# Attention's block mask: written into PSUM by VectorE, in place of a product of mask tiles on TensorE

## The chip, the cores and the metric

The kernel runs on one core of one Trainium2 chip. A core has TensorE (matrix products, PE in the profile; PEld is its weight loads), VectorE (DVE), ScalarE (ACT), GpSimd (POOL) and SyncE (SP), which issues most of the loads. TensorE writes into PSUM, which VectorE and ScalarE read and write; the other operands lie in SBUF. The metric is device time in microseconds (us) from start to end of one execution; less is better.

## The reference

Two layers of a streaming encoder on x of shape (1, 1024, 1024). The first mixes by a gated short convolution, the second by latent attention with 8 heads; each is followed by a squared-ReLU MLP of 4096. What matters here is the attention with its mask. Queries come in blocks of 128 rows and see keys in chunks of 64: a row of chunk c sees chunks 0 to c.

```python
for i in range(S // Q_BLOCK):
    q0, k_end = i * Q_BLOCK, (i + 1) * Q_BLOCK
    ...
    q_chunk = np.arange(q0, k_end) // CHUNK
    k_chunk = np.arange(k_end) // CHUNK
    mask = k_chunk[None, :] <= q_chunk[:, None]
    s = jnp.where(mask[None, None], s, jnp.finfo(jnp.float32).min)
    p = jax.nn.softmax(s, axis=-1).astype(v.dtype)
    outs.append(jnp.einsum("bhqk,bkhd->bqhd", p, v[:, :k_end]))
```

With Q_BLOCK 128 and CHUNK 64, keys beyond the block are never computed, and of the keys of a block's own 128 columns only one square is masked: the first 64 rows of the block do not see its last 64 columns.

## The kernel before

All large products are split into a high and a low part, and three products of such parts stand for one (`mm`, line 173). The program's stages follow each other: convolution layer, its MLP, the shared keys and values, attention, output projection, second MLP. Attention runs from about 1145 to 1431 us of the profile.

Attention loops over the heads h = 0 to 7, and in each over blocks i = 7 down to 0 of 128 queries. `scores(i, ...)` computes one block for one head into `sp`, a PSUM tile of up to 1024 columns (two banks, named big in the profile, of which there are two). For each bank of 512 columns there are five products (line 1433): rotary and plain parts, high and low. Then one more product is added onto the last 64 columns (line 1434). Its operands are two constant tiles: `mask_l`, 128 x 128, of which row 0 is 1 in columns 0 to 63, and `mask_r`, 128 x 64, of which row 0 is -2^127. It adds -2^127 to the first 64 rows of the last 64 columns and 0 to the others. VectorE takes the negated row maximum (line 1436), ScalarE the exponential with its row sum (line 1439), and `end()`, called later, the reciprocal of the sum and the scaling of the row (lines 1443 and 1444). The scaled rows p are turned by TensorE (`turn`, transposes on line 1459), evicted in a high part by ScalarE (1462) and a low part by VectorE (1463), and multiplied with the values.

Between the blocks stand the keys, queries, rotary parts and values of the next head, and the modulation sums of the second layer (`ada_acc`, line 198 on VectorE, which add up rows of a weight as they are loaded).

The source sets the order of the calls. In stretches marked `pinned` it is kept on the engines; elsewhere, in attention too, a planner orders each engine's instructions by what is ready in its own reckoning, with the source's order as priority.

`mask_l` and `mask_r` are filled once, by two casts (lines 1103 and 1104) from `cs`, a tile of constants loaded at the start (line 136), which also holds the identity for the transposes. The host writes the constants (`_consts`): identity, the two mask pieces, then the tables of cosines and sines.

Of the kernel before, what the change touches and what calls it, by code (L numbers as in the profile page):

```python
# [9 lines left out]
F32R = mybir.dt.float32r  # L10
# [7 lines left out]
P = 128  # L18
# [4 lines left out]
HALF = 512  # L23
CHUNK = 64
# [9 lines left out]
MASKED = -(2.0 ** 127)  # L34
# [19 lines left out]

VEC_ROWS = 109
BIAS_ROWS = 112
C_ID, C_ML, C_MR, C_T = 0, 128, 256, 320
C_COLS = 2368


@with_exitstack
def trunk_kernel(ctx: ExitStack, tc: tile.TileContext, x, c, ada_w, ada_b, norm_g, conv_in_w, conv_w,
                 conv_b, conv_out_w, kv_ada_w, kv_ada_b, kv_norm_g, kv_a_w, kv_a_norm_g, kv_b_w,
                 q_a_w, q_a_norm_g, q_b_w, attn_o_w, mlp_up_w, mlp_down_w, consts, out):
    nc = tc.nc
    uid = [0]

    def nm(s):
        uid[0] += 1
        return f"{s}_{uid[0]}"  # L70

    def pool(name, side="left", **kw):
        return tc.alloc_tile_pool(name=name, bufs=1, side=side, reuse_waits="tile", **kw)

    cp = pool("cp")
# [24 lines left out]
    def big_ps():  # L100
        return wide[0].tile([P, 2 * HALF], F32, tag="big", name=nm("big"))
# [4 lines left out]
    def small(w=1):  # L106
        return cp.tile([P, 8], F32, tag="small", name=nm("small"), bufs=16)[:, :w]
# [22 lines left out]
    cs = cp.tile([P, C_T], F32, name="cs")  # L130
# [33 lines left out]
        return vecs[:, (l * 4 + v) * 8:(l * 4 + v) * 8 + 8]  # L164

    V_CW, V_CB, V_KV, V_QA, V_KA = 64, 88, 96, 104, 107

    mask_l = cp.tile([P, P], F32R, name="mask_l")
    mask_r = cp.tile([P, CHUNK], F32R, name="mask_r")

    def mm(out_, lhs, rhs, first, last, more=False):
        for i, (a, b) in enumerate(((1, 0), (0, 1), (0, 0))):
# [740 lines left out]
    def conv_phase():  # L913
# [77 lines left out]
        def weights(k, m):  # L991

            raw = ad.tile([P, D], F32, tag=("acc", "gmb")[k % 2], name=nm("w"), bufs=1)[:, :3 * P]
            ld(raw.rearrange("p (g m) -> p g m", g=3),
               conv_in_w[0][k * P:(k + 1) * P, :].rearrange("p (g c) -> p g c", g=3)[:, :, m * P:(m + 1) * P])
            w = [wr.tile([P, 3 * P], F32R, tag="w" + part_, name=nm("w"), bufs=6) for part_ in "hl"]
            split_w(w[0], w[1], raw)
            return w
# [56 lines left out]
        with pinned([mybir.EngineType.PE, mybir.EngineType.SP]):  # L1055
            load_x(0)
            aw = [ada(0)]
            w = [weights(0, 0)]
# [27 lines left out]
            w = w[KD]  # L1086
# [7 lines left out]
            for k in range(KD):  # L1094
                w, w_ = weights(k + 1, 1) if k < KD - 1 else None, w
# [4 lines left out]
            evict(1, acc)  # L1100
        wr.release()
        up = pool("up", "right")
        nc.vector.tensor_copy(mask_l, cs[:, C_ML:C_ML + P])
        nc.vector.tensor_copy(mask_r, cs[:, C_MR:C_MR + CHUNK])

        def triple(j):
            keep = {}
# [44 lines left out]
    bg += ada_fm(ad, "s0f", w0, 4 * D, 32, gain(0, 2))  # L1152
    bg += ada_fm(ad, "h0f", w0, 3 * D, 24)
    conv_phase()

    def down_phase(slots, sizes, wd, src_fn, g, xsrc, xdst, next_w, key, ys=None, pairs=True):
# [262 lines left out]
    def scores(i, K, Q, r_):  # L1419

        n = (i + 1) * P
        qs = slice((i % 4) * P, (i % 4 + 1) * P)
        q = Q[i // 4]
        r_ = r_[i // 4]
        sp = big_ps()
        for b in range((n + HALF - 1) // HALF):
            w = min(HALF, n - b * HALF)
            o_ = sp[:, b * HALF:b * HALF + w]
            kp = [t_[:, b * HALF:b * HALF + w] for t_ in kk]
            ops = [(r_[:, qs], kp[1]), (q[1][:, qs], K[b][0][:, :w]), (r_[:, qs], kp[0]), (q[0][:, qs], K[b][1][:, :w]),  # L1430
                   (q[0][:, qs], K[b][0][:, :w])]
            for j, (a, m_) in enumerate(ops):
                nc.tensor.matmul(o_, a, m_, start=j == 0, stop=j == 4 and b * HALF + w < n)  # L1433
        nc.tensor.matmul(sp[:, n - CHUNK:n], mask_l, mask_r, start=False, stop=True)
        mx = small()
        nc.vector.tensor_reduce(mx, sp[:, :n], AX.X, ALU.max, negate=True)
        pt = at.tile([P, n], F32, tag=f"p{i}", name=nm("p"), bufs=1)
        l_ = small()
        nc.scalar.activation(pt, sp[:, :n], AF.Exp, bias=mx, accum_out=l_)

        def end():
            rl = small()
            nc.vector.reciprocal(rl, l_)
            nc.vector.tensor_scalar(pt, pt, rl, None, op0=ALU.mult)

        return pt, end
# [56 lines left out]
    for h in range(H):  # L1503
# [5 lines left out]
        run_bg(5)  # L1509
        pts = {}  # L1510
        pts[7], end = scores(7, K, Q, r_)
        if before:
            before.turn(2)
        else:
            values(V, kw0, 0)
            values(V, kw0, 1)
        end()
        pts[6], end = scores(6, K, Q, r_)
        if before:
            before.turn()  # L1520
            before.mul(3)
        else:
            values(V, kw0, 2)
            values(V, kw0, 3)
        end()
        pts[5], end = scores(5, K, Q, r_)
        if more:
            qw_ = q_weights(raw_q, h + 1)
# [77 lines left out]
def _consts():  # L1606
    import numpy as np
    k = np.zeros((P, C_COLS), np.float32)
    k[:, C_ID:C_ID + P] = np.eye(P)
    inv = (np.float32(1.0) / np.power(np.float32(10000.0), np.arange(0, ROPE, 2, dtype=np.float32) / np.float32(ROPE)))  # L1610
    ang = np.arange(S, dtype=np.float32)[None, :] * inv.astype(np.float32)[:, None]
    cos, sin = np.cos(ang).astype(np.float32), np.sin(ang).astype(np.float32)
    k[:, C_T:C_T + S] = np.concatenate([cos] * 4)
    k[:, C_T + S:] = np.concatenate([-sin, sin] * 2)
    k[0, C_ML:C_ML + CHUNK] = 1.0
    k[0, C_MR:C_MR + CHUNK] = MASKED
    return k


# [20 lines left out]
```

## Time and profile before

| what | value |
|---|---|
| three runs | median 2179.61 us, 2178.7 to 2180.36 |
| the profiled execution | 2180.9 us |
| its span, first to last instruction | 2179.1 us |
| mean granted TensorE clock | 0.993 |

The page gives busy time by engine, the span in slices, the DMA queues, the chain of work that ended last, and the costliest groups of instructions. In a row such as "L1436 DVE TENSOR_REDUCE small<-big" stand the source line, the engine, the operation, and the tiles written and read. "x64 | 42.8, 686 | 7.8 <-ACT pt L1462 7.6" are the number of instructions, their busy time in us, the mean length of one in ns, and the idle time of the engine just before them with what ended most of it. A row of the timeline has start, length, engine, line, operation; a row of the chain has start, length on the chain, engine and line. "ACT p L1439 <- DVE small L1436" is a row of the waits: who waited for whom, us in total, times, longest.

### The profile page before, as it was taken

The page shows a single profiled execution, that of the slowest core. Times are in us where ns is not written, and L with a number is a line of the kernel's source. Part 1 is how long each engine was busy: PE and PEld are TensorE (multiplying, and loading weights), DVE is VectorE, ACT ScalarE, POOL GpSimd, SP SyncE. Part 2 cuts the span into 40 slices and gives each one's busy share as a digit, 9 for nine tenths or more (in the row PEclk, how much of TensorE's full clock was granted, in tenths as well). Part 3 has the DMA queues.
Part 4 walks back from the last instruction along what each step waited for, and adds up shares of the span by engine and source line. Part 5 has one row for each costly group of instructions (what it writes and reads, how often), then busy time and mean ns, then how long its engine had stood idle before and what let it go on. Part 6 is the DMA issues. An engine that isn't in the chain of part 4 may idle for free.

```text
span 2179.1 us, 25354 instructions
## 1 busy us (share of the span) xinstructions
PE 2098.4 (96%) x9702; PEld 1726.9 (79%) x9702; DVE 1512.0 (69%) x2001; ACT 1062.7 (49%) x1512; POOL 4.0 (0%) x8
## 2 busy tenths in 40 slices
PE   6999999989999999999899999999989999999998
PEld 5888878768888778888777888877768887788887
DVE  5877776967665578956788776665966665458556
ACT  4533354735454434344665555564735444444342
POOL 0000000000000000000000000000000000000000
PEclk9999999999999999999999999999999999999999
DMA  8344463346543977444224131053345553853243
GB/s 243 101 147 134 145 212 127 101 146 203 184 160 120 330 262 254 167 147 170 78 69 122 66 113 44 25 164 122 98 149 174 183 188 119 312 196 126 97 145 135
DMA packets 242335, 330.95 MB, mean 152 GB/s; under 512 B 18629, under 2 KB 143906, under 8 KB 242214
## 3 DMA queue, kind: packets, MB, share of 16 engines
q1 hardware_dynamic: 204328, 248.57, 35.8%
q10 hardware_dynamic: 37886, 80.77, 9.8%
q8 instruction: 76, 1.25, 0.2%
q14 instruction: 45, 0.37, 0.1%
HBM read 248.55 MB, written 80.74 MB: 151 GB/s over the span
## 4 chain that ended last, share of the span: by engine, by line
PE 69%; DVE 14%; ACT 8%; DMA 6%; issue 2%; SPq 0%; ACTq 0%; DVEq 0%
PE one L173 34%; PE mm L173 18%; PE tp L173 7%; PE big L173 4%; DMA raw<-in_ada_w_dram 3%; ACT junk L258 2%; PE big L1433 2%; DVE y L318 1%; DVE raw L319 1%; DVE acc L198 1%; PE tp L1459 1%; DVE uplo L177 1%; DMA raw<-ha 1%; DVE y L312 1%; ACT small L260 1%
## 5 line engine op out<-in xcount | busy, mean ns | idle before, releaser
L173 PE MATMUL one<-slot,uphi 128*128 128x512 f32 x1240 | 383.9, 391 | 0.0
L173 PEld LDWEIGHTS one<-slot,uphi 128*128 128x128 f32 x1240 | 233.8, 189 | 48.6 <-issue 0.5
L173 PE MATMUL big<-slot 128*128 128x512 f32 x1152 | 266.5, 391 | 1.0 <-ACT y L884 0.6
L173 PE MATMUL one<-slot,uplo 128*128 128x512 f32 x620 | 244.1, 394 | 14.6 <-DVE y L580 12.6
L173 PEld LDWEIGHTS big<-slot 128*128 128x128 f32 x1152 | 215.9, 188 | 46.7 <-ACT y L884 1.4
L173 PE MATMUL one<-ring,ring 128*128 128x512 f32 x1008 | 232.3, 391 | 6.5 <-DVE ring L177 6.5
L177 DVE TENSOR_TENSOR uplo<-raw,uphi 128x1024 fp32r<-128x1024 f32 x121 | 145.8, 1221 | 130.5 <-ACT uphi L176 130.5
L176 ACT ACTIVATE ring<-w 128x1024 fp32r<-128x1024 f32 x98 | 103.7, 1058 | 261.7 <-PE tp L173 132.1
L173 PEld LDWEIGHTS one<-ring,ring 128*128 128x128 f32 x1008 | 188.2, 188 | 49.5 <-ACT ring L176 5.8
L176 ACT ACTIVATE uphi<-raw 128x1024 fp32r<-128x1024 f32 x121 | 128.2, 1060 | 143.8 <-PE one L173 91.6
L177 DVE TENSOR_TENSOR ring<-w,ring 128x1024 fp32r<-128x1024 f32 x98 | 119.8, 1222 | 109.7 <-ACT ring L176 109.6
L173 PE MATMUL mm<-ring,ring 128*128 128x512 f32 x672 | 162.4, 390 | 0.0
L173 PE MATMUL tp<-ring,ring 128*128 128x512 f32 x672 | 161.7, 389 | 0.0
L173 PE MATMUL mm<-slot,uphi 128*128 128x512 f32 x504 | 158.5, 395 | 0.0
L173 PEld LDWEIGHTS one<-slot,uplo 128*128 128x128 f32 x620 | 116.8, 188 | 43.6 <-DVE y L580 15.1
L173 PEld LDWEIGHTS mm<-ring,ring 128*128 128x128 f32 x672 | 125.7, 188 | 27.1 <-DVE ring L177 0.6
L173 PEld LDWEIGHTS tp<-ring,ring 128*128 128x128 f32 x672 | 126.2, 188 | 26.2
L198 DVE SCALAR_TENSOR_TENSOR acc<-raw,csil,acc 128x1024 f32<-128x1024 f32 x88 | 112.8, 1282 | 45.7 <-DMA raw<-in_ada_w_dram 42.2
L177 DVE TENSOR_TENSOR ring<-raw,ring 128x1024 fp32r<-128x1024 f32 x98 | 119.4, 1219 | 18.3 <-ACT ring L176 18.3
L173 PE MATMUL one<-slot,s 128*128 128x512 f32 x468 | 115.1, 395 | 3.7 <-DVE s L177 3.7
L578 ACT ACTIVATE y<-one 128x512 f32<-128x512 f32 x62 | 36.7, 592 | 159.3 <-PE one L173 104.7
L173 PEld LDWEIGHTS mm<-slot,uphi 128*128 128x128 f32 x504 | 95.3, 190 | 20.3 <-issue 1.4
(278 smaller groups left out, 3498.4 us busy)
## 6 DMA issues: line engine op xcount, KB each, us to landing
ha<-y ACTq DMA_DIRECT2D x196, 256.0 KB, 3.6
raw<-ha SPq DMA_DIRECT2D x98, 512.0 KB, 4.2
raw<-in_ada_w_dram SPq DMA_DIRECT2D x80, 512.0 KB, 4.5
raw<-in_mlp_up_w_dram SPq DMA_DIRECT2D x70, 512.0 KB, 4.2
w<-in_mlp_down_w_dram SPq DMA_DIRECT2D x56, 512.0 KB, 4.9
raw<-hd SPq DMA_DIRECT2D x24, 512.0 KB, 5.3
xs<-raw ACTq DMA_DIRECT2D x24, 512.0 KB, 2.9
raw<-xs SPq DMA_DIRECT2D x24, 512.0 KB, 3.2
```

The source lines that it names most:

```text
L173: nc.tensor.matmul(out_, lhs[a], rhs[b], start=first and i == 0, stop=last and i == 2, skip_group_check=more)
L176: nc.scalar.activation(hi, src, AF.Copy)
L177: nc.vector.tensor_tensor(lo, src, hi.bitcast(F32), op=ALU.subtract)
L198: nc.vector.scalar_tensor_tensor(acc, raw, s, acc, op0=ALU.mult, op1=ALU.add)
L258: nc.scalar.activation(junk, src, AF.Square, accum_out=ss)
L260: nc.scalar.activation(rt, ss, AF.Sqrt, bias=eps_d)
L312: nc.vector.tensor_tensor(y, y, p_, op=ALU.add)
L318: nc.vector.scalar_tensor_tensor(y, y, rroot(ss), self.gmb, op0=ALU.mult, op1=ALU.mult)
L319: nc.vector.tensor_tensor(xr, xr, y, op=ALU.add)
L578: nc.scalar.activation(dst, x_, AF.Copy)
L1433: nc.tensor.matmul(o_, a, m_, start=j == 0, stop=j == 4 and b * HALF + w < n)
L1459: nc.tensor.transpose(p_[:, c:c + P], pts[4 * hf + i][:, j * P:(j + 1) * P], ident)
```

## The change

The product on line 1434 goes. In its place VectorE writes -2^127 into the masked square (64 rows, the last 64 columns) of the scores in PSUM, after the products and ahead of the row maximum. The two mask tiles, their casts and their place in the constants go too, so that `cs` has 128 columns instead of 320. Which of the five products carries the stop mark changes with it.

```diff
-C_ID, C_ML, C_MR, C_T = 0, 128, 256, 320
-C_COLS = 2368
+C_ID, C_T = 0, 128
+C_COLS = 2176
...
-    mask_l = cp.tile([P, P], F32R, name="mask_l")
-    mask_r = cp.tile([P, CHUNK], F32R, name="mask_r")
...
-        nc.vector.tensor_copy(mask_l, cs[:, C_ML:C_ML + P])
-        nc.vector.tensor_copy(mask_r, cs[:, C_MR:C_MR + CHUNK])
...
             for j, (a, m_) in enumerate(ops):
-                nc.tensor.matmul(o_, a, m_, start=j == 0, stop=j == 4 and b * HALF + w < n)
-        nc.tensor.matmul(sp[:, n - CHUNK:n], mask_l, mask_r, start=False, stop=True)
+                nc.tensor.matmul(o_, a, m_, start=j == 0, stop=j == 4)
+        nc.vector.memset(sp[:CHUNK, n - CHUNK:n], MASKED)
         mx = small()
         nc.vector.tensor_reduce(mx, sp[:, :n], AX.X, ALU.max, negate=True)
...
-    k[0, C_ML:C_ML + CHUNK] = 1.0
-    k[0, C_MR:C_MR + CHUNK] = MASKED
```

## The prediction

> **What bounds the kernel now.** I read the head of the page and its chain, then the busy time by stage, then the lines of the mask, then single instructions around them.
>
> ```profile
> span 2179.1 us, 25354 instructions
> PE 2098.4 (96%) x9702; PEld 1726.9 (79%) x9702; DVE 1512.0 (69%) x2001; ACT 1062.7 (49%) x1512; POOL 4.0 (0%) x8
> PE 69%; DVE 14%; ACT 8%; DMA 6%; issue 2%; SPq 0%; ACTq 0%; DVEq 0%
> ```
>
> The kernel is bound by TensorE: 96% busy, 69% of the chain that ended last. The change touches one stage, attention, and a few instructions in the first microseconds. The busy time by stretch (us busy, instructions in brackets; PE, PEld, DVE, ACT, POOL) shows attention whole, its first head, and an inner head:
>
> ```profile
> 1145.00:1431.00 286.00, 274.27 (x1579) 232.63 (x1578) 215.00 (x385) 157.34 (x315) 0.00 (x0) 1.00 0.22 71
> 1145.00:1170.00 25.00, 20.72 (x121) 17.57 (x119) 24.81 (x36) 14.73 (x25) 0.00 (x0) 1.00 0.47 136
> 1232.00:1263.00 31.00, 30.76 (x182) 26.69 (x181) 22.48 (x44) 16.74 (x34) 0.00 (x0) 1.00 0.10 32
> ```
>
> Attention lasts 286 us. The inner head is TensorE's (30.76 of 31). The first head is VectorE's (24.81 of 25). So the change, which takes work from TensorE and gives work to VectorE, gains in some places and loses in others, and the sum has to be made place by place on the chain.
>
> **What is removed on TensorE.** The answer for the line of the mask product:
>
> ```profile
> L1434 PE MATMUL big<-mask_r,mask_l x64: 191/193/246, 1152.0 to 1430.5; 128*128 128x64 f32 x64
> ```
>
> There are 64 products, eight in each of eight heads. Their 193 ns is a latency. What they cost a stream is seen from one start to the next. TensorE alone, narrow stretches of the timeline (start us, length us):
>
> ```profile
> 1238.59 0.19 PE L1434 MATMUL big<-mask_r,mask_l 128*128 128x64 f32 x1
> 1238.62 0.47 PE L173 MATMUL mm<-ckT,kw 128*128 128x512 f32 x1
> 1238.93 0.39 PE L173 MATMUL mm<-ckT,kw 128*128 128x512 f32 x1
> 1239.16 0.40 PE L173 MATMUL mm<-ckT,kw 128*128 128x512 f32 x1
> ...
> 1245.12 0.19 PE L1434 MATMUL big<-mask_r,mask_l 128*128 128x64 f32 x1
> 1245.15 0.30 PE L1459 MATMUL tp<-cs,p 128*128 128x128 f32 x1
> 1245.29 0.38 PE L1459 MATMUL tp<-cs,p 128*128 128x128 f32 x2
> 1247.75 0.60 PE L1459 MATMUL tp<-cs,p 128*128 128x128 f32 x4
> ```
>
> The product behind the mask starts 0.03 us after it, but the one after that only 0.31 later, where the ordinary step of these 512-column products is 0.23 (1238.93 to 1239.16). So a mask costs 0.03 + 0.31 - 0.23 = 0.11 us: a 64-column product is too short to hide the next weight load. Ahead of a transpose it costs 0.03 + 0.14 - 0.11 = 0.06 us, the ordinary step of transposes being (0.60 - 0.38) / 2 = 0.11, from the rows of four and of two.
>
> The Trainium skill, TensorE: Matmul & The Clock Gate, section Part 2 (step 1, and the table under Back-to-back issue gap), has the next weights load while the present product runs, and a product of up to 64 columns at about 60 cycles with a floor near 25 ns. The trace agrees for the start of the next product and not for the one after it. An estimate by that page is 34 x 25 ns = 0.9 us where the rows below give 3.1.
>
> The chain inside attention passes through the mask product 34 times; first and last:
>
> ```profile
> 1172.20 0.03 PE big L1434
> ...
> 1425.52 0.03 PE big L1434
> ```
>
> Of these, 20 stand ahead of a wide product and 14 ahead of a transpose (counted in the timeline): 20 x 0.11 + 14 x 0.06 = 3.0 us gained. The other 30 lie where TensorE waits for something else soon after, or is behind another engine, and I take them at nothing. If all 54 whose next product starts within 0.1 us counted (34 wide, 20 transposes), the gain would be 34 x 0.11 + 20 x 0.06 = 4.9 us; that is the upper end.
>
> **What is added on VectorE.** Sixty-four memsets of 64 x 64 into PSUM, each right ahead of a row maximum. The trace has no memset into PSUM. The nearest rows are the memsets into SBUF, and the row maximum itself, which touches PSUM:
>
> ```profile
> L154 DVE MEMSET ones<- x1: 165/165/165, 0.8 to 0.8; 128x128 f32 x1
> L156 DVE MEMSET eps_d<- x1: 59/59/59, 0.9 to 0.9; 128x1 f32 x1
> ...
> L1436 DVE TENSOR_REDUCE small<-big 128x1 f32<-128x256 f32 x8 | 3.3, 409 | 0.0
> L1436 DVE TENSOR_REDUCE small<-big 128x1 f32<-128x128 f32 x8 | 2.3, 282 | 0.0
> ```
>
> Between the memset rows, 64 columns take 59 + 63 x 106 / 127 = 112 ns; that is the value I take, being the same operation. Above, the maximum shrunk to 64 columns takes 282 - 127 / 2 = 219 ns. Below, 59 ns. The maximum reads what the memset writes, so it waits for it. What such a pair and a free pair cost:
>
> ```profile
> 1237.08 0.16 DVE L1443 RECIPROCAL small<-small 128x1 f32<-128x1 f32 x1 [0.17 <-ACT p L1439]
> 1237.28 0.69 DVE L1444 TENSOR_SCALAR p<-p,small 128x896 f32<-128x896 f32 x1
> ...
> 1241.58 0.68 DVE L1387 TENSOR_TENSOR k<-mm,k 128x512 fp32r<-128x512 f32 x1
> 1242.18 0.81 DVE L1436 TENSOR_REDUCE small<-big 128x1 f32<-128x640 f32 x1
> ```
>
> A dependent instruction starts 0.04 us after the end of the one before (1237.24 to 1237.28), an independent one 0.08 before it (1242.26 to 1242.18). The memset takes the maximum's old place behind the earlier work, so it puts the maximum back by 0.11 + 0.04 = 0.15 us; at the upper bound 0.26; at the lower end, 59 ns overlapped by 0.08, nothing. The chain passes through the maximum 21 times, and that is where it counts; the first, and groups in which it stands between a reciprocal and its scaling, the first and last of seven (the last is the last maximum too):
>
> ```profile
> 1154.81 0.98 DVE small L1436
> ...
> 1159.47 0.07 DVE small L1443
> 1159.54 0.99 DVE small L1436
> 1160.53 0.66 DVE p L1444
> ...
> 1422.05 0.16 DVE small L1443
> 1422.21 0.59 DVE small L1436
> 1422.80 0.47 DVE p L1444
> ```
>
> So 21 x 0.15 = 3.2 us lost; bounds 0 and 21 x 0.26 = 5.5 us. At the other 43 the cover is VectorE's idle time in the stage, 286 - 215 = 71 us; without that cover all 64 would cost 9.6 us. Behind the waiting memset stand the maximum, the reciprocal and scaling of the tile before, and the splits of the turned tiles; ScalarE's exponential waits for the maximum, and TensorE's transposes for the scaling.
>
> The Trainium skill, VectorE: DVE Perf Modes, section The TRN2 errata, gives an operation from PSUM 120 cycles plus one per element at 0.96 GHz, which would be 192 ns here if writing to PSUM costs the same. An estimate by that page is 21 x (0.19 + 0.04) = 4.8 us in place of 3.2. No row of this trace shows the operation.
>
> **What moves at the start.** Two casts go, and the first load carries 128 columns instead of 320.
>
> ```profile
> L1103 DVE CAST mask_l<-cs x1: 227/227/227, 3.2 to 3.2; 128x128 fp32r<-128x128 f32 x1
> L1104 DVE CAST mask_r<-cs x1: 186/186/186, 3.4 to 3.4; 128x64 fp32r<-128x64 f32 x1
> ...
> 7.42 0.17 DVE L180 TENSOR_SCALAR csil<-csil 128x8 f32<-128x8 f32 x1 [3.86 <-ACT csil L151]
> 8.38 0.41 PE L936 MATMUL tp<-cs,raw 109*128 109x109 f32 x1 [8.38 <-DMA raw<-in_kv_a_norm_g_dram]
> ```
>
> VectorE idles 3.86 us behind the casts, and TensorE's first product waits for another load until 8.38. Nothing is gained; without that cover it would be the 0.4 us of the two casts. The tiles behind move by 1.5 KB in each partition, which I put at nothing, as the size of no tile that is worked on changes.
>
> **Sum.** -3.0 + 3.2 = +0.2 us, which is no change. The profiled execution took 2180.9 us, 1.8 outside its span, and lies 1.3 above the median of the runs shown, 2179.61. On the profiled execution the sum is 2181.1, on the median 2179.8. With both bounds the case reaches from -4.9 to -3.0 + 5.5 = +2.5: 2174.7 to 2182.1.
>
> **The rivals.** The casts stand at 3.2 us although their line comes after the convolution: the order on an engine is set by a planner that works with its own times, not by the source. That is where the other cases come from.
>
> Slower, by one mechanism: something is put between the memset and its maximum. The planner does so with the reciprocal and its scaling whenever other work is ready (seven of the 21 places above). The piece it would find most often is a split of a turned tile:
>
> ```profile
> L1463 DVE TENSOR_TENSOR pt<-tp,pt 128x512 fp32r<-128x512 f32 x64 | 42.8, 686 | 7.8 <-ACT pt L1462 7.6
> ...
> ACT p L1439 <- DVE small L1436: 43.2, 39, 2.1
> DVE acc L198 <- DMA raw<-in_ada_w_dram: 8.0, 6, 3.1
> ```
>
> Each such place puts the exponential back by 0.69 us, and ScalarE already waits 43.2 us for the maxima, 39 times. At seven places on the chain that is 4.8 us, with the sum above +5.0: 2184.6; at ten, +7.1: 2186.7. It decides from seven places (4.4 us is 0.2%). Against it: where the chain is pure VectorE work, the order inside it costs nothing.
>
> Faster: the memsets fall into the pauses that dependent pairs leave, and cost nothing on the chain, and the shifted order spares the modulation sums one of their waits for a load (last row: 8.0 us in six waits, longest 3.1). Then -3.0 - 3.1 = -6.1: 2173.5. For it: in the group at 1159.47 a memset could stand in the reciprocal's shadow. Against it: these waits hang on buffers that VectorE itself frees, and later work frees them later.
>
> The mask was cheap: the weight load behind it is hidden after all, the longer step after it has another cause that stays, and a mask is worth only its 0.03 us. Then 34 x 0.03 = 1.0 us are gained, and the sum is +2.2: 2181.8. The rows at 1238.62 and 1238.93 speak against it, since the longer step stands behind the mask and not one product later. This is how the Trainium skill's page TensorE: Matmul & The Clock Gate, quoted above, would have it.
>
> **How the numbers follow.** Forecast 0.46; slower 0.29; faster 0.22; the cheap mask 0.03. A measurement of this kernel can tell about 0.2%, 4.4 us, from no change. The forecast and the cheap mask fall within it: faster 0.22, same 0.49, slower 0.29. The predicted time is the forecast's, 2179.8. The range takes in the faster case and the slower one at ten places: 2173.0 to 2187.0; the likeliest case's own is 2174.7 to 2182.1.
>
> **What would show it.** Right: no mask product; 64 memsets of 0.09 to 0.2 us; the wide product behind a score block stepping at 0.23 at once; inner heads (1232 to 1263) shorter by 0.5 us or so, the first head longer by up to 1; attention still 285 to 288 us. Wrong: memsets over 0.26 us; other work between memset and maximum at seven or more places of the chain; waits of the modulation sums for loads far from 8.0 us; or stages outside attention moving by over 1 us.

## The result, and the profile after

The changed kernel takes 2172.81 us (median of 9 runs, 2169.01 to 2176.85), the kernel before 2178.81 us (9 runs, 2175.83 to 2181.37) beside it: a ratio of 0.9974, 95% interval [0.9964, 0.9983], or 6.0 us less. That is faster than no change by more than the 0.2% that can be told apart. The forecast was no change, 2179.8, and its range began at 2173.0, so the result lies 0.2 us below it.

The profiled execution of the changed kernel took 2172.25 us. The head of its page and the line of the chain by engine:

```profile
span 2170.5 us, 25290 instructions
PE 2087.5 (96%) x9638; PEld 1713.6 (79%) x9638; DVE 1518.0 (70%) x2063; ACT 1061.3 (49%) x1512; POOL 4.0 (0%) x8
PE 69%; DVE 15%; ACT 8%; DMA 5%; issue 2%; ACTq 0%; SPq 0%; DVEq 0%
```

TensorE has 64 instructions less, VectorE 62 more (64 memsets, two casts less). Line numbers have moved: the row maximum is line 1431 now, the memset 1429, the score products 1428, the reciprocal and scaling 1438 and 1439, the low parts of the turned tiles 1458, the modulation sums 195.

To find where the time went I cut attention at the first row maximum of each head (the 1024-column one) and read the busy time by stretch. The eighth row ends at the last transposes, the ninth is everything behind. The kernel before:

```profile
core 0: us, PE busy (x) PEld busy (x) DVE busy (x) ACT busy (x) POOL busy (x), PEclk, DMA share, GB/s
1154.73:1188.27 33.54, 30.95 (x170) 25.21 (x170) 27.54 (x50) 15.93 (x32) 0.00 (x0) 1.00 0.32 96
1188.27:1231.84 43.57, 41.00 (x238) 34.57 (x237) 35.36 (x60) 24.81 (x49) 0.00 (x0) 1.00 0.37 121
1231.84:1263.76 31.92, 31.68 (x188) 27.48 (x187) 22.81 (x46) 16.85 (x35) 0.00 (x0) 1.00 0.11 36
1263.76:1306.13 42.37, 41.04 (x240) 34.85 (x239) 35.48 (x59) 24.61 (x49) 0.00 (x0) 1.00 0.38 125
1306.13:1337.99 31.86, 31.62 (x186) 27.25 (x185) 21.98 (x43) 16.97 (x35) 0.00 (x0) 1.00 0.08 25
1337.99:1380.10 42.11, 41.06 (x238) 34.82 (x237) 27.81 (x52) 24.71 (x49) 0.00 (x0) 1.00 0.16 58
1380.10:1410.17 30.07, 29.83 (x172) 25.69 (x171) 19.79 (x39) 15.17 (x33) 0.00 (x0) 1.00 0.05 18
1410.17:1440.63 30.46, 27.61 (x152) 23.05 (x151) 22.09 (x40) 17.52 (x34) 0.00 (x0) 0.94 0.22 70
1440.63:2179.08 738.45, 716.19 (x3165) 587.67 (x3163) 475.56 (x556) 348.84 (x445) 0.95 (x1) 1.00 0.47 160
```

The kernel after, cut in the same way:

```profile
1153.87:1188.19 34.32, 31.74 (x170) 25.22 (x171) 28.99 (x57) 16.02 (x34) 0.00 (x0) 1.00 0.33 103
1188.19:1228.87 40.68, 39.79 (x227) 33.03 (x226) 35.54 (x68) 24.54 (x49) 0.00 (x0) 1.00 0.38 121
1228.87:1260.18 31.31, 30.52 (x180) 26.31 (x179) 22.93 (x54) 16.18 (x34) 0.00 (x0) 1.00 0.12 40
1260.18:1302.67 42.49, 40.70 (x230) 33.87 (x230) 36.73 (x70) 25.03 (x50) 0.00 (x0) 1.00 0.38 122
1302.67:1333.41 30.74, 29.96 (x175) 25.74 (x174) 22.24 (x50) 15.86 (x33) 0.00 (x0) 1.00 0.08 27
1333.41:1374.42 41.01, 40.42 (x235) 34.10 (x234) 29.17 (x61) 25.12 (x50) 0.00 (x0) 1.00 0.16 58
1374.42:1403.99 29.57, 28.79 (x159) 24.03 (x158) 20.23 (x47) 14.34 (x32) 0.00 (x0) 1.00 0.05 19
1403.99:1432.30 28.31, 25.70 (x143) 20.66 (x142) 22.64 (x47) 17.32 (x34) 0.00 (x0) 1.00 0.19 61
1432.30:2170.45 738.15, 716.23 (x3165) 587.73 (x3163) 475.72 (x556) 348.76 (x445) 0.96 (x1) 1.00 0.47 161
```

Behind attention nothing moved (738.45 and 738.15). The first cut comes 0.9 us earlier than before, which says little: over the profiled runs below it comes between 1151 and 1156. The first seven heads went from 255.4 to 250.1 us, -5.3, with the largest piece, -2.9, in head 1. Head 7 shows -2.2, but its mean clock was 0.94 before and 1.00 after; in two more profiles of the changed kernel (e14 and e12) it took 29.7 and 29.9 us at 0.94, so some 1.5 us of this is the clock of one execution.

The waits in attention in the kernel after (who waited for whom: us in total, times, longest) beside the rows of before in the prediction:

```profile
ACT p L1434 <- DVE small L1431: 36.8, 29, 2.1
...
DVE big L1429 <- PE big L1428: 6.1, 7, 1.4
...
DVE acc L195 <- DMA raw<-in_ada_w_dram: 1.7, 2, 1.1
```

The exponential waits 36.8 us for maxima instead of 43.2, and the modulation sums wait 1.7 us for their loads instead of 8.0. Not every wait fell: ScalarE's wait for the transposes went from 37.4 to 41.5 us. Whether the swap or something else did this is tested below. On VectorE, the memset's group, and then the timeline of one stretch of head 2:

```profile
L1429 DVE MEMSET big<- x64: 112/112/112, 1153.2 to 1424.5; 64x64 f32 x64
```

```profile
1231.35 0.16 DVE L1438 RECIPROCAL small<-small 128x1 f32<-128x1 f32 x1
1231.52 0.11 DVE L1429 MEMSET big<- 64x64 f32 x1
1231.55 0.75 DVE L1439 TENSOR_SCALAR p<-p,small 128x1024 f32<-128x1024 f32 x1
1232.22 1.08 DVE L1431 TENSOR_REDUCE small<-big 128x1 f32<-128x896 f32 x1
...
1234.47 0.16 DVE L1438 RECIPROCAL small<-small 128x1 f32<-128x1 f32 x1 [0.83 <-ACT p L1434]
1234.74 0.11 DVE L1429 MEMSET big<- 64x64 f32 x1
1234.77 0.62 DVE L1439 TENSOR_SCALAR p<-p,small 128x896 f32<-128x896 f32 x1
...
1237.36 0.17 DVE L1438 RECIPROCAL small<-small 128x1 f32<-128x1 f32 x1 [0.19 <-ACT p L1434]
1237.57 0.62 DVE L1439 TENSOR_SCALAR p<-p,small 128x768 f32<-128x768 f32 x1
1238.19 0.11 DVE L1429 MEMSET big<- 64x64 f32 x1
1238.34 0.83 DVE L1431 TENSOR_REDUCE small<-big 128x1 f32<-128x640 f32 x1
```

A memset lasts 112 ns, always. Right ahead of its maximum it costs 0.15 us (1238.19 to 1238.34). Between a reciprocal and the scaling that needs it, it can cost nothing: the scaling starts 0.04 us after the reciprocal's end in the upper lines, with a memset between, and in the lower, without. In the middle lines it does cost: there the memset itself waits 0.11 us for its score products, and the scaling starts 0.14 us after the reciprocal. Twenty of the 64 memsets stand in such a pause, 21 right ahead of their maximum, the rest ahead of other work; of the twenty, 16 leave the scaling where it was and four waited like this one.

The two programs' instruction streams differ by more than the edit. SyncE and GpSimd have the same order, and so have all engines outside attention, but in attention 159 instructions of VectorE, 522 of TensorE and 69 of ScalarE stand at another place. The planner has ordered the stage anew.

### The profile page after: what moved, and what is told of

Read it like the earlier page. It is cut to its first block, busy times and chain, and to the rows that moved or that the text cites. A ratio compares the mean times of both kernels' runs of the same rounds, so it can differ in the third digit from the quotient of the medians.

```text
span 2170.5 us, 25290 instructions
## 1 busy us (share of the span) xinstructions
PE 2087.5 (96%) x9638; PEld 1713.6 (79%) x9638; DVE 1518.0 (70%) x2063; ACT 1061.3 (49%) x1512; POOL 4.0 (0%) x8
## 4 chain that ended last, share of the span: by engine, by line
PE 69%; DVE 15%; ACT 8%; DMA 5%; issue 2%; ACTq 0%; SPq 0%; DVEq 0%
PE one L170 35%; PE mm L170 18%; PE tp L170 7%; PE big L170 4%; ACT junk L255 2%; DMA raw<-in_ada_w_dram 2%; PE big L1428 2%; DVE y L315 1%; DVE raw L316 1%; DVE acc L195 1%; PE tp L1454 1%; DVE uplo L174 1%; DVE y L309 1%; DMA raw<-ha 1%; ACT small L257 1%
```

## The experiments

So there are two suspects: the swap of operations, and the new order. **Theory A**: the order is the gain. **Rival B**: the swap is the gain, through the mask products that are gone. To part them, a helper holds attention's instructions on TensorE, VectorE and ScalarE in an order read from a list, that of before or that of after; whatever is not shared (mask product, memset) is put at a named place: the product behind the last score product, the memset right ahead of its maximum.

```diff
+    def keep_order():
+        ...
+        for e_, steps in PLAN:                       # engine, places
+            seq = [...]                              # its instructions in that order
+            for x_, y_ in zip(seq, seq[1:]):
+                tc.add_manual_dep(y_, x_.name, NO_SYNC, reason="kept order")
+    keep_order()
```

This adds an order, and no instruction. A run with neither operation leaves the mask out, so that it serves as a price only. In the table below, "heads 2, 4, 6" is the time of these three heads in the profiled execution, cut as above (before 93.9, after 91.6). They hardly hold modulation sums (one addition in head 2), and the clock was 1.00 in them in these runs; it serves to compare operations in one order.

**Operation against order.** The diffs are the helper, and the two lines with or without:

```diff
 (e1) -mask product  +memset   PLAN of before
 (e2)  mask product            PLAN of after
 (e3) -mask product            PLAN of before
 (e4)  mask product  +memset   PLAN of before
 (e5) -mask product            PLAN of after
 (e6)  mask product  +memset   PLAN of after
```

Memsets in the order of before:

> The change (memsets, no mask products), with the instructions of attention held on every engine in the order that the planner had given the kernel before; each memset stands right ahead of its row maximum. Theory A, the gain of 6 us is the planner's new order: nothing or at most 2 us is left of it here, since 34 masks at about 0.09 us are paid back by 21 memsets at 0.15 us. Theory B, the gain is that of the instructions, and the memsets lie in pauses of VectorE: 3 to 6 us faster than the kernel before, about as fast as the kernel after.

Mask products in the order of after:

> The kernel before (mask products, no memsets), with attention held in the order that the planner gave the kernel after. Theory A: 4 to 6 us faster than the kernel before. Theory B: within 1 us of it. If both have a part, 2 to 4 us faster.

Neither, in the order of before:

> Neither mask products nor memsets (the mask is left out), attention held in the order of the kernel before. It prices the mask products alone. By the sum of the prediction 3.0 us faster than the kernel before (34 on the chain), at most 4.9 (all 54 that are not followed by a wait). Theory B needs 5 to 6 here.

Both, in the order of before:

> Mask products and memsets, attention held in the order of the kernel before. It prices the memsets alone. By the sum of the prediction 3.2 us slower than the kernel before (21 on the chain at 0.15 us). Theory B: within 1 us of it, the memsets being hidden.

Neither, in the order of after:

> Neither mask products nor memsets (the mask is left out), attention held in the order of the kernel after. It prices the mask products in that order. If they cost there what they cost in the order before (about 4 us), this is 10 to 12 us faster than the kernel before. If TensorE has more slack in that order, 7 to 9.

Both, in the order of after:

> Mask products and memsets, attention held in the order of the kernel after. It prices the memsets in that order. Theory: that order was planned with memsets, so that they stand where a dependent pair leaves a pause, and cost 3 to 5 us in place of the 8 they cost in the order before: 2 to 4 us faster than the kernel before. Rival: a memset costs about 8 us in either order, and only the mask products differ: about 1 us slower than the kernel before.

| run | operation | order | ratio to before [95%] | heads 2, 4, 6 |
|---|---|---|---|---|
| e1 | memset | before | 1.0037 [1.0026, 1.0047] | 97.0 |
| e2 | mask product | after | 0.9968 [0.9957, 0.9979] | 90.2 |
| e3 | neither | before | 0.9980 [0.9971, 0.9990] | 92.4 |
| e4 | both | before | 1.0039 [1.0024, 1.0054] | 97.6 |
| e5 | neither | after | 0.9965 [0.9953, 0.9978] | 89.1 |
| e6 | both | after | 1.0017 [1.0008, 1.0026] | 93.1 |

Rival B falls twice: the swap alone makes the kernel slower by 0.37%, 8 us (e1), and the new order alone, with all mask products kept, makes it faster by 0.32%, 7 us (e2). The waits fell with the order too, with no memset in the kernel; in e2 they are:

```profile
ACT p L1453 <- DVE small L1450: 31.5, 25, 1.8
...
DVE acc L209 <- DMA raw<-in_ada_w_dram: 2.1, 2, 1.1
```

The prices follow. Alone, a mask product is worth (93.85 - 92.44) / 24 = 59 ns over three heads of eight blocks in the old order, 48 ns in the new ((90.25 - 89.09) / 24); all 64 some 3 to 4 us, and e3 has 4.4 by its ratio (3.0 by the medians). A memset right ahead of its maximum in the old order is worth (97.0 - 92.4) / 24 = 0.19 us, all 64 some 12 us. The two prices do not add up: with the mask products kept, the memsets cost 8.5 us (e4), and with the memsets there, all the mask products and their two casts cost only 0.4 us by the ratios and 1.6 by the medians (e4 against e1). Beside the memsets, VectorE had become the engine to wait for. The waits and the chain of e1 show it:

```profile
ACT p L1446 <- DVE small L1442: 53.5, 44, 2.3
```

```profile
1151.08 0.12 DVE big L1440
...
1436.77 0.12 DVE big L1440
```

The exponential waits 53.5 us for the maxima (43.2 before), and the chain, which in the kernel before went through 21 maxima, goes through 47 in e1, first and last memset on it shown.

Several results lie outside what was expected: e1 lost 8 us where a gain of up to 6 was expected, e4 lost 8.5 where 3.2 was, and e6 lost 3.7, more than the 1 of its rival. All three have the memset right ahead of its maximum, which is dearer than was thought. The gain of e2 is a little over its 4 to 6; e3 and e5, with 4.4 and 7.6 us, came out as expected.

**The planner by itself**, both operations or neither, no order held:

```diff
 (e7) mask product, +memset, no PLAN
 (e8) -mask product, no PLAN
```

> Mask products and memsets, order left to the planner. Theory: it is the memset between the scores and the row maximum that makes the planner choose the better order, so that the kernel before with 64 memsets added and nothing taken away is faster by 2 to 4 us. Rival: the missing product brings the order about; then this is about as slow as the memsets in the order before, 6 to 9 us slower.

> Neither mask products nor memsets (the mask is left out), order left to the planner. Theory: without the memset the planner stays near the order before, and the gain is that of the products alone, 3 to 5 us. Rival (the missing product brings the better order): 9 to 12 us faster.

Both: 1.0002 [0.9992, 1.0011]. Neither: 0.9973 [0.9963, 0.9983]. Neither range expected of e7 held, and e8 gained 5.9 us, a little over its 3 to 5. With both operations the planner comes, on VectorE, to an order near that of after and to no loss, where both held to the order of before lost 0.39%. With neither, it stays nearer to that of before. Counted in the traces, without telling buffers apart, VectorE's order in e7 differs at 39 places from after and at 144 from before, in e8 at 133 and 82. So it is the added memset rather than the missing product that leads the planner to that order. It does not get all of it: on TensorE, e7 lies as far from after (225 places) as from before (216).

**Which part of the order.** The additions of the modulation sums stand later in the new order, and wait less for their loads. With mask products throughout: sums moved alone (e9), all but the sums (e10), about the first half of attention only (e11, e18).

```diff
 (e9)  PLAN of before, acc additions behind the same instructions as in after
 (e10) PLAN of after, acc additions behind the same instructions as in before
 (e11) PLAN of after, then of before: VectorE from the middle of head 3, ScalarE
       from head 4, TensorE from the second block of head 4
 (e18) the same, on all three from the first block of head 4
```

> Mask products, everything in attention in the order of before, except the additions of the modulation sums on VectorE, which stand behind the same instructions as in the order of after (later in heads 1 to 2 and 4 to 5). Theory 'late sums' (the new order gains because the sums no longer wait for their loads, 8.0 us before, 1.7 after): ratio 0.997 to 0.998, waits of the sums for loads about 2 us. Rival 'block order' (the gain comes from the order of score blocks, turned tiles and splits): 0.999 to 1.001, even if the waits for loads fall.

> Mask products, everything in attention in the order of after, except the additions of the modulation sums, which stand behind the same instructions as in the order of before. 'Late sums': the waits for loads come back (about 8 us) and the ratio goes to 0.999 to 1.000. 'Block order': 0.997 stays, as with the whole order of after.

> Mask products; the first four heads in the order of after, the last four in that of before, on all three engines. Whole order of after: 0.9968. If the gain is spread evenly over the heads (per-block order), 0.998 to 0.999; if it is made by the sums, of which the longest waits stand in heads 1 and 2, 0.997; if it is in the last heads, 1.000.

> Mask products; heads 0 to 3 in the order of after, heads 4 to 7 in that of before, cut on each engine at the first block of head 4 (score products on TensorE, row maximum on VectorE, exponential on ScalarE). The run with half of the order before this one was cut in the middle of head 3 on VectorE, at the second block of head 4 on TensorE and at the end of head 3 on ScalarE, so its loss may be the seam's. If the order's gain is local to the heads: heads 0 to 3 as with the whole order of after (149.6 us instead of 151.4), heads 4 to 7 as before, ratio 0.998 to 0.9995. If the order only works as a whole: 1.000 or over, with heads 3 or 4 longer again.

| run | ratio to before [95%] | head 0 | 1 | 2 | 3 | 4 | 5 | 6 |
|---|---|---|---|---|---|---|---|---|
| before | 1 | 33.5 | 43.6 | 31.9 | 42.4 | 31.9 | 42.1 | 30.1 |
| e2, whole order of after | 0.9968 | 34.5 | 40.7 | 30.6 | 43.8 | 30.5 | 41.6 | 29.1 |
| e9 | 1.0018 [1.0009, 1.0026] | 37.9 | 42.1 | 31.9 | 42.6 | 31.9 | 42.1 | 30.0 |
| e10 | 1.0015 [1.0005, 1.0024] | 34.2 | 45.8 | 30.9 | 47.2 | 30.9 | 41.5 | 29.2 |
| e11 | 1.0010 [1.0001, 1.0018] | 34.5 | 40.8 | 30.5 | 44.9 | 33.8 | 42.1 | 30.0 |
| e18 | 1.0004 [0.9994, 1.0013] | 34.5 | 40.7 | 30.5 | 43.2 | 35.2 | 42.1 | 30.1 |

None of the expectations of e9, e10 and e11 held: three mixtures are slower than either whole, and the fourth, e18, lies level with before, where its second expectation had it. The cut of e11 was also not where its expectation says, but at three different places, which is why e18 was run. The heads say what happened. The waits of the sums for loads, in e9 and in e10:

```profile
DVE acc L208 <- DMA raw<-in_ada_w_dram: 2.9, 3, 1.7
```

```profile
DVE acc L209 <- DMA raw<-in_ada_w_dram: 11.7, 6, 3.2
```

With the early sums put back into the new order (e10), heads 1 and 3 grow by 5.1 and 3.4 us (up to half of the 3.4 is a clock of 0.96 in head 3), and the waits come back as 11.7 us. So the new order needs its late sums; that no other order gains with early sums isn't shown. They aren't enough: in the old order (e9) head 1 gains 1.5 us, but head 0, where its sums now stand in the way, loses 4.4 (with a clock of 0.95 in that stretch). With half of the order and one clean cut (e18), heads 0 to 3 keep their gain, 148.9 us against 151.4, and head 4 loses it: 35.2 against 31.9, of which a drop of the clock has up to 1.7 (in e11, at a clock of 1.00, head 4 takes 33.8). By its ratio nothing is left of the gain. It seems that what the new order leaves for later in head 3 has to be done in head 4. So a head that is shorter is not yet a gain, since work crosses the cut (the third row of before has 188 products, of after 180 and no masks; e2 has 182 with them): between two orders only the whole stage can be compared, and single heads only between runs of one order. The order's 7 us are there with the whole of it.

**What the swap is worth in the new order**: the changed kernel again (e12), and mask products in its order once more (e13) beside the changed kernel (e14).

```diff
 (e12, e14) the changed kernel
 (e13) mask product, PLAN of after, as e2
```

> The changed kernel itself, on the chip of this call, for comparison with the mixed orders beside it: 0.9974 again, within 0.001. It should lie level with mask products in its own order (0.9968), or up to 1 us above them if the swap by itself costs something in the new order.

> Mask products in the order of after, beside the changed kernel in one call, for what the swap itself costs or brings in the new order. By the durations of heads 2 and 4 (mask products 30.6 and 30.5 us, memsets 31.3 and 30.7) it should be 0.5 to 2 us faster than the changed kernel: ratio 0.9965 to 0.997. Rival: the swap is worth its 3 to 4 us of mask products in the new order too, and this kernel is slower than the changed one, 0.998 to 0.999.

> The changed kernel beside it: 0.9974 to 0.9977 as before. If the swap costs something in the new order, it lies 0.5 to 2 us above the kernel with mask products in the same order; by the rival 2 to 4 us below it.

e12: 0.9977 [0.9969, 0.9986]. e13: 0.9973 [0.9962, 0.9984]; e14 on the same chip: 0.9981 [0.9972, 0.9990]. The kernel with mask products is 0.9 us faster by the medians, but the intervals overlap: the swap in the new order is worth nothing that can be told. That it still gains 3 to 4 us there is not borne out. The eight rows of attention, added up in four profiles, show what cancels: 285.9 us before, 279.0 with the order alone (e2), 276.0 with the mask products gone too (e5), 278.4 with the memsets (after). So the order brings 6.9 us, of which up to 1.7 is the lower clock in head 7 of before, the mask products 3.0, and the memsets take 2.4 back. No version was found that surely beats the changed kernel.

**Why the swap is free there and costs 8 us in the old order.** The changed kernel doesn't have its memsets right ahead of the maxima. Here "free" is the swap as a whole. Theory "shadow": a memset costs what its place costs, nothing behind a reciprocal. Rival: the order of all else decides. Only the memsets move now: right ahead of the maxima in the order of after (e15), and one instruction earlier where a reciprocal or a scaling stands ahead of them, in the order of before (e16) and of after (e17).

```diff
 (e15) +memset right ahead of its maximum, PLAN of after
 (e16, e17)
+            for k_ in range(1, len(seq)):
+                if seq[k_].name in sets and type(seq[k_ - 1]).__name__ in EARLY:
+                    seq[k_ - 1], seq[k_] = seq[k_], seq[k_ - 1]
```

> Memsets, the order of after for all else, but each memset right ahead of its maximum instead of where the changed kernel has it (there 20 of 64 stand between a reciprocal and its scaling, which starts 35 ns after the reciprocal with the memset between them or without). Theory 'shadow' (what a memset costs is set by its place: nothing in the pause behind a reciprocal, 0.15 us right ahead of the maximum): 20 x 0.15 = 3 us and up to 43 x 0.15 = 6.5 us above the changed kernel, ratio 0.999 to 1.0005. Rival 'order alone': 0.9974 to 0.998, as the changed kernel.

> Memsets in the order of before, but each one instruction earlier where the instruction ahead of it is a reciprocal or a scaling (38 or so of 64 places): between the reciprocal and its scaling, or ahead of a reciprocal that then stands between memset and maximum. 'Shadow': most of the 0.15 us goes at these places, 3 to 6 us less than with the memsets right ahead of the maximum (1.0037): 1.0010 to 1.0023. 'Order alone': 1.003 to 1.0045.

> The same in the order of after: each memset one instruction earlier than right ahead of its maximum, where a reciprocal or a scaling stands there (some 42 of 64 places). 'Shadow': as the changed kernel or a little better, 0.997 to 0.998. 'Order alone': 0.9974 to 0.998 for this kernel and the one with adjacent memsets alike.

e15: 1.0014 [1.0004, 1.0023], 2180.99 us, a little more than the shadow theory's range; e17: 0.9981 [0.9973, 0.9990], 2174.93 us, as the changed kernel. In the new order the place of the memsets alone is worth 6 us by the medians. The same stretch of head 2 as above, in e15:

```profile
1238.44 0.16 DVE L1451 RECIPROCAL small<-small 128x1 f32<-128x1 f32 x1 [0.35 <-ACT p L1447]
1238.64 0.62 DVE L1452 TENSOR_SCALAR p<-p,small 128x768 f32<-128x768 f32 x1
1239.26 0.11 DVE L1441 MEMSET big<- 64x64 f32 x1
1239.41 0.82 DVE L1443 TENSOR_REDUCE small<-big 128x1 f32<-128x640 f32 x1
```

The pause of 0.04 us between reciprocal and scaling stays empty, and 0.15 us stand ahead of the maximum. Most of the loss against the changed kernel, 4.6 of 5.1 us over seven heads, is in heads 0, 1, 3 and 5 (35.3, 41.7, 44.2 and 41.8 us). Heads 0, 1 and 3 are those in which VectorE adds the sums as well.

In the old order the shadow theory fails: e16 took 2189.23 us, 1.0046 [1.0033, 1.0058], no better than e1. There 18 of the memsets stood in a reciprocal's pause already: in that order the maximum itself fills it, as at 1159.47 in the prediction's rows, and a memset takes the maximum's place in it. Moved earlier, it waits for the score products instead. The waits in e1 and in e16:

```profile
DVE big L1440 <- PE big L1439: 8.5, 10, 1.4
```

```profile
DVE big L1441 <- PE big L1440: 18.0, 14, 3.0
```

VectorE stands still for 18.0 us behind waiting memsets instead of 8.5. So a memset is free where the order leaves a pause behind work that is due anyway and the scores are there; both came with the new order. Not all 64 are free there: in the changed kernel heads 2, 4 and 6 take 91.6 us, and 89.1 without memsets (e5), 0.1 us for each, while heads 0, 1, 3 and 5 together lose nothing.

## Why the prediction was wrong

**The step that failed first** is the assumption under the whole sum: that attention keeps its order, so that the change can be costed at the places of the chain of before. The prediction knew that a planner sets the order and used it for its rivals only, at 0.51 of the chance. With that order held, the swap costs 8 us (e1) instead of +0.2; with the planner free, the new order alone brings 7 us (e2; 6 when run again, e13), and the swap in it nothing that can be told.

**Mask products, -3.0 us with 4.9 as the upper end**: right for the mask products alone. e3 gives 4.4 us (interval 2.2 to 6.3), and the heads 59 ns each over all blocks, where 3.0 and 4.9 us are 47 and 77 ns. (The 3.1 that the prediction sets beside the page's estimate is this same sum of 3.0.) But the prediction added this gain to the loss on VectorE, both worked out on the chain of before, and in that order the two do not add: once the memsets were there, 0.4 to 1.6 us of the gain were left (e1 against e4). The 512-column products behind a score block now step by 0.23 to 0.24 us at once, as it said:

```profile
1242.44 0.52 PE L1428 MATMUL big<-k,q 128*128 128x384 f32 x2
1242.80 0.40 PE L170 MATMUL mm<-pt,v 128*128 128x512 f32 x1
1243.04 0.40 PE L170 MATMUL mm<-ckT,kw 128*128 128x512 f32 x1
1243.27 0.62 PE L170 MATMUL mm<-pt,v 128*128 128x512 f32 x2
```

The cheap mask, 1.0 us in all, is outside e3's interval. The Trainium skill's page TensorE: Matmul & The Clock Gate, which the prediction set beside it, has the floor near 25 ns in the table under Back-to-back issue gap, and says there that this isolated gap under-counts at small N, since it leaves out the weight loads. The 59 ns per product here agree with that reservation.

**Memsets, 112 ns and 0.15 us in place**: right to the nanosecond and to the hundredth. The Trainium skill's page VectorE: DVE Perf Modes, section The TRN2 errata, gives its 120 cycles for operations from PSUM to SBUF. That writing into PSUM costs as much, which would have made 192 ns, is not borne out by the memset here.

**21 of them on the chain, the other 43 covered by idle time of 71 us: +3.2**: this is the term that was mis-sized. In the order it was made for, the memsets cost about 12 us without the mask products (e1 against e3: 2185.9 against 2174.43, one chip) and 8.5 with them (e4), on either side of the 9.6 the prediction gave for "without cover". An idle share of 25% was no cover, since the idle time lay in other places than the maxima: the chain simply moved onto VectorE, from 21 maxima to 47. A count of places on the chain of before holds only while the added time is small against the slack beside the chain, and with 0.15 us a block it was not. Why e1 comes to 0.19 us a block, more than the 0.15 in place, isn't shown.

**The wrong signs it listed.** Other work between memset and maximum at seven or more places of the chain: at 12 of 20. First and last memset on the chain of the changed kernel:

```profile
1153.25 0.11 DVE big L1429
...
1410.72 0.12 DVE big L1429
```

The slower rival expected this sign to cost 0.69 us a place, a split between the two. What the planner put there on the chain was the scaling at four places, an addition of the modulation sums at four, a split at two and other work at two; over all blocks it was the scaling in 20 of 43 cases. So the sign came, and the splits that were to carry its price were rare; the kernel got faster all the same, since the places came with a new order. The waits of the sums "far from 8.0" are there too, at 1.7. Stages outside attention did not move: 738.45 against 738.15 us behind it. Of the right signs, the product stepping at 0.23, the inner head shorter by 0.6 us and the first longer by 0.8 came true; attention at 285 to 288 us did not, since the eight rows went from 285.9 to 278.4.

**The faster rival, 2173.5 us at 0.22,** had the mechanism: memsets in the pauses of dependent pairs, and a shifted order that spares the sums their waits. It put this at -3.0 for the masks and -3.1 for one wait. The total of -6.1 is close to the measured -6.0, which is in part luck, since the shares differ: with the masks kept, the order alone brings 6 to 7 us, and the memsets aren't free in all heads. Its counter-argument, that later work frees the buffers later, did not decide.

What stays open: which exchanges within the new order bring its 7 us. The late sums are needed for them; the runs show that they aren't enough, and that half of the order brings nothing.

## What to carry to other kernels

Where a planner orders a stage, an edit is two changes, the operation and the order that it brings about; hold the order in one run and the operation in another before crediting either. A short instruction on an engine that others wait for is priced by its place: count the pauses between dependent pairs that are still empty, since idle time elsewhere on that engine is no cover. Prices found one at a time need not add up: a gain on one engine can vanish when the same edit makes another engine the slower one. A gain that is only the order's can be had without the edit, as the mask products in the new order showed.

## What the runs showed of the hardware

A memset of 64 x 64 into PSUM took 112 ns in all 64 cases, what the two memsets into SBUF of 128 and 1 columns give for 64 columns. Between a reciprocal and the scaling that reads its result VectorE has a pause of 35 ns, into which an independent memset of 112 ns fits in 16 of 20 cases with a delay of at most 8 ns: the scaling starts some 80 ns before the memset's end. In the other four the memset waited 97 to 122 ns for score products, and the scaling began 126 to 151 ns after the reciprocal. So an instruction that doesn't depend on its neighbours can cost less than its own duration.

The granted clock falls to 0.50 for 3.4 us at a time, in attention in some executions and not in others, with either order and either operation: in e18 from 1302.46 to 1305.87, in head 4. As the mean of a head of 30 to 45 us this reads as 0.94 to 0.96. In the last head it made 28.3 us of the changed kernel into 29.7 and 29.9. A difference of 1 to 2 us in one stretch between two profiles should be read with that column beside it.
